# The third feed-forward's first product by seven block products instead of eight, with sums of weight blocks on GpSimd and sums of results when banks are read

## The chip, the cores and the metric

One core of one Trainium2 chip runs the whole program. The metric is the device time in microseconds (us) from start to end of one execution; the median of several executions counts. TensorE (PE in the profile) multiplies, with its weight loads listed apart as PEld; VectorE is DVE, ScalarE is ACT, GpSimd is POOL, and SyncE (SP) issues the loads from HBM. SBUF is the on-chip memory that all engines read, PSUM holds the eight banks into which TensorE writes its products.

## What is computed

Two layers over 256 context tokens and 256 latent tokens of 1024 features. Each layer is a feed-forward (FFN), a token mixer, and a second FFN; every part has a normalisation with shift, scale and gate in front. The change concerns the first FFN of the second layer, the third of four:

```python
def _modulated_norm(h, gain, shift, scale):
    return _rms_norm(h, gain) * (1.0 + scale) + shift

def _swiglu(h, w1, w2):
    a, b = jnp.split(h @ w1, 2, axis=-1)
    return (jax.nn.silu(a) * b) @ w2

for i in range(DEPTH):
    mx = (cond_x @ ada_w[i] + ada_b[i]).reshape(n_batch, 3, 3, 1, d)
    x = x + FFN_RESIDUAL * mx[:, 0, 2] * _swiglu(
        _modulated_norm(x, norm_g[i, 0], mx[:, 0, 0], mx[:, 0, 1]), ffn_w1[i, 0], ffn_w2[i, 0])
    ...
```

`w1` has 1024 rows and 2 x 2816 columns, so `h @ w1` gives 22 blocks of 128 columns for `a` and 22 for `b`. Inputs and weights are fp32.

## The kernel before

**Tiling.** Activations lie with features on the 128 partitions and all 512 tokens in a row: context in columns 0 to 255 (`CTX`), latent in 256 to 511 (`LAT`). The normalised input `H` is eight such chunks (k = 0 to 7). To keep fp32 accuracy each operand of a product is split into a rounded part "hi" and a rest "lo", and each product of two chunks is three matmuls: hi by hi, hi by lo, lo by hi (`mm3`, L292). A pair of outputs (`pa` for a block of `a`, `pb` for the same block of `b`, one PSUM bank each) takes 2 x 8 chunks x 3 = 48 matmuls of 512 columns (`ffn1_pairs`, L996).

**Weights.** `plan_weights` (L306) lists all weight loads and units in the order of use. SyncE loads tiles of 1024 rows by 256 columns into two pools of two buffers (`raw` and `ub`). `_split` (L447) makes a unit's hi by a ScalarE copy and its lo by a VectorE subtraction, four chunks (128x512) at a time. `w_ahead` (L483) is a task that keeps `LOOK` = 4 units split ahead of use. A unit of the FFN's first product is eight chunks, so a pair costs four copies and four subtractions.

**Evacuation.** `ffn_evac` (L871) reads a finished pair: silu of `pa` on ScalarE, times `pb` on VectorE, a rounded copy on ScalarE, the rest on VectorE. The result chunks `G` are the inputs of the second product (`out_blocks`, L1053), which adds each output block to the residual by VectorE.

**Order of the work.** An FFN runs in three parts of 6, 8 and 8 pairs, each followed by its share of the second product (`ffn`, L1102). The first two pairs of part 0 run as two halves by token group (`halves_first`, L1014), context columns first, because the normalisation of the latent half (`norm_half`, L856, and `h_chunks`, L817) ends later. A recording scheduler (`Sched`, L69) fixes the order of the instructions on every engine: each engine's queue is in program order, and tasks such as weight splits, evacuations and `ada_gen` (L682, the modulation vectors: 16 steps for each vector, here first eight VectorE steps, then eight ScalarE steps with seven GpSimd additions) are put in between matmuls by a clock that the scheduler keeps from its own costs. All recorded vector, scalar and GpSimd instructions carry line L184, the matmuls L284 and the transposes L289. In the names of the profile `u` is any tile of a pool of 76 buffers of 128x512 fp32, `mm` a PSUM bank, `raw` and `ub` loaded weights, `cc` the conditioning vector of `ada_gen`.

Of the kernel before, what the change touches and what calls it, by code (L numbers as in the profile page):

```python
# [213 lines left out]
class Kernel:  # L214
# [3 lines left out]
    LAG = (0.0, 2000.0)  # L218

    def __init__(self, tc, a, out, dbg, stack):  # L220
        self.s = Sched()
# [49 lines left out]

    def mm(self, out, lhsT, rhs, start=True, stop=True, tp=None, ns=None):
        kw = {} if tp is None else {"tile_position": tp}
# [10 lines left out]
        self.nc.tensor.matmul(out, lhsT, rhs, start=start, stop=stop, **kw)  # L284
        self.s.tick(ns)
# [6 lines left out]
    def mm3(self, ps, w, h, nk, sl=ALL, ks=None, start=True, stop=True):  # L292
# [4 lines left out]
        for i, k in enumerate(ks):  # L297
            if h is self.H:
                self.h_wait(k, sl)
            wh, wl = whi[k // 4][:, k % 4, :], wlo[k // 4][:, k % 4, :]  # L300
            self.mm(ps[:, sl], wh, hhi[k][:, sl], start=(start and i == 0), stop=False)
# [4 lines left out]
    def plan_weights(self):  # L306
# [13 lines left out]
        def unit(r, views, shape):  # L320
            for i in r:
                self.raws[i]["left"] += 1
            self.units.append({"r": r, "views": views, "shape": shape, "w": None})

# [8 lines left out]
        def ffn1(w1, p0, n):  # L333
# [33 lines left out]
        for l in range(2):  # L367
            for j in range(2):
                w1, w2 = a["ffn_w1"][l, j], a["ffn_w2"][l, j]
                for p0, n in self.parts:  # L370
                    if first:
                        ffn1(w1, 3, 3)
                        first = False
                    else:
                        ffn1(w1, p0, n)
# [71 lines left out]
    def _split(self):  # L447
        un = self.units[self.u_split]
        nc = self.nc
        tiles = [self.raws[i]["tile"] for i in un["r"]]  # L450
        nk, w = un["shape"]
        hi, lo = [], []
        if w == 512:
# [27 lines left out]
        self.u_split += 1  # L481

    def w_ahead(self):  # L483
# [333 lines left out]
    def h_chunks(self, hf, l, slot, ks, pace=None):  # L817
# [16 lines left out]
        for k in ks:  # L834
# [9 lines left out]
            f = None  # L844
            if k % 2:
                f = self.u()
# [9 lines left out]
    def norm_half(self, hf, sq, l, slot):  # L856
# [7 lines left out]
        if hf == "x":  # L864
            self.tables("silu")
            self.norming = self.urgent = self.lo_mix = False
            if (l, slot) == (0, 2):
                self.ada_pause = self.ada_hold = False


    def ffn_evac(self, pa, pb, sl):  # L871
# [230 lines left out]
    def ffn(self, l, j, sl, nxt, start=False):  # L1102
        v = 8 if j else 2
        for pi, (p0, n) in enumerate(self.parts):
            self.G = ([], [])
            if pi == 2 and (l, j) == (0, 0):
                self.ada_hold = True
            if pi == 0:
# [15 lines left out]
            else:
                self.ffn1_pairs(n, sl)
            last = pi == 2
# [848 lines left out]
    def run(self, upto=None):  # L1975
        self.upto = upto
        nc = self.nc
        self.acc = self.rs = None
        self.table = None
# [65 lines left out]
```

## Time and profile before

| | us |
|---|---|
| median of 3 runs (lowest, highest) | 1926.26 (1923.22, 1930.32) |
| the profiled execution, its own time | 1926.65 |
| span of its trace | 1924.9 |
| the third FFN's stretch with 512 columns at a time | 1232 to 1553 |

The profiled execution lies 0.39 us above the median, and its span covers all but 1.75 us of its time. In the views, a row of the timeline gives start, duration, engine, line, operation, output and input tiles, the count of merged instructions and, in brackets, the idle time before them and who ended it. A row by windows gives the length of the window, and for each engine its busy time and count of instructions, then the granted TensorE clock. A row of groups gives busy time, mean duration in ns, and the idle time before the instructions.

### The profile page before, as it was taken

The numbers are of one execution on the slowest core, as the hardware profiler recorded it, in microseconds if no ns is written. First come the engines' busy times: TensorE is split into PE (matmuls) and PEld (weight loads), VectorE is DVE, ScalarE is ACT, GpSimd is POOL, SyncE is SP. The second block draws the span as 40 slices with busy tenths as digits, with TensorE's granted clock in tenths as the row PEclk, the third lists the DMA queues.
The fourth block names the chain that finished last, engine by engine and source line by source line (L and its number), as shares of the span: only waits on it lengthen the run. The fifth ranks groups of instructions, "written<-read, shape, count | busy, mean of one in ns | idle before, by whom it ended". The sixth has DMA issues, their size and how long they took to land.

```text
span 1924.9 us, 28979 instructions
## 1 busy us (share of the span) xinstructions
PE 1865.4 (97%) x10719; PEld 1526.7 (79%) x10719; DVE 1282.2 (67%) x2124; ACT 965.4 (50%) x2106; POOL 643.6 (33%) x594
## 2 busy tenths in 40 slices
PE   8999999999999999999999999999999999899998
PEld 5878888897776666788888889888888898687887
DVE  4887877755977965478787786655433355956565
ACT  4544534457566455465445444533422248866553
POOL 3343433344546435354344333311200047230000
PEclk8999999999999998999999999999999999999999
DMA  9655554413322242444555454455323425126551
GB/s 290 211 184 194 179 175 153 129 46 125 94 67 83 69 162 83 151 157 157 193 187 170 159 197 147 142 175 187 119 91 102 131 67 110 45 67 184 199 197 66
DMA packets 238708, 271.70 MB, mean 141 GB/s; under 512 B 12343, under 2 KB 189135, under 8 KB 238567
## 3 DMA queue, kind: packets, MB, share of 16 engines
q1 hardware_dynamic: 237703, 269.15, 43.2%
q8 instruction: 84, 1.38, 0.3%
q10 hardware_dynamic: 720, 0.59, 0.1%
q14 instruction: 57, 0.47, 0.1%
q0 software_dynamic: 144, 0.11, 0.0%
HBM read 259.32 MB, written 10.49 MB: 140 GB/s over the span
## 4 chain that ended last, share of the span: by engine, by line
PE 56%; DVE 7%; ACT 4%; issue 2%; DMA 1%; POOL 1%; DVEq 0%; ACTq 0%; POOLq 0%
PE mm L284 55%; DVE u L184 6%; ACT u L184 3%; PE mm L289 1%; POOL u L184 1%; DMA raw<-in_ffn_w 0%; DVE st L184 0%; DVE big L184 0%; DMA ub<-in_ffn_w 0%; DMA u<-XD 0%; DVE ub L184 0%; ACT L184 0%; ACT ub L184 0%; ACT sc L184 0%; DVEq L184 0%
## 5 line engine op out<-in xcount | busy, mean ns | idle before, releaser
L284 PE MATMUL mm<-u 128*128 128x512 f32 (+4 forms) x9480 | 1777.0, 353 | 25.3 <-POOL u L184 9.9
L284 PEld LDWEIGHTS mm<-u 128*128 128x128 f32 (+1 forms) x9480 | 1457.4, 185 | 329.3 <-issue 39.6
L184 POOL TENSOR_TENSOR u<-u 128x512 f32<-128x512 f32 (+4 forms) x386 | 426.1, 1110 | 916.4 <-ACT u L184 869.8
L184 ACT ACTIVATE u<-u 128x512 fp32r<-128x512 f32 (+8 forms) x361 | 171.0, 485 | 450.5 <-DVE u L184 435.9
L184 ACT ACTIVATE u<-mm 128x128 f32<-128x128 f32 (+5 forms) x382 | 151.4, 412 | 252.3 <-PE mm L284 169.9
L184 DVE TENSOR_TENSOR u<-raw,u 128x512 fp32r<-128x512 f32 (+2 forms) x270 | 218.3, 849 | 63.2 <-ACT u L184 63.1
L184 DVE SCALAR_TENSOR_TENSOR u<-u,cc 128x512 f32<-128x512 f32 x196 | 222.5, 1135 | 10.1 <-DMA u<-in_ada_w 6.9
L184 DVE TENSOR_TENSOR u<-ub,u 128x512 fp32r<-128x512 f32 x252 | 199.1, 832 | 29.6 <-ACT u L184 29.5
L184 ACT ACTIVATE u<-raw 128x512 fp32r<-128x512 f32 (+1 forms) x372 | 206.3, 607 | 18.7 <-DMA raw<-in_ffn_w 11.8
L184 ACT ACTIVATE u<-u,cc 128x512 f32<-128x512 f32 x224 | 151.7, 711 | 112.4 <-DMA u<-in_ada_w 108.5
L184 POOL TENSOR_TENSOR u<-raw,u 128x512 fp32r<-128x512 f32 x98 | 129.6, 1347 | 141.8 <-ACT u L184 109.4
L184 ACT ACTIVATE u<-ub 128x512 fp32r<-128x512 f32 (+1 forms) x282 | 156.4, 609 | 18.4 <-DVE u L184 8.2
L184 DVE TENSOR_TENSOR u<-u,mm 128x512 f32<-128x512 f32 x66 | 45.2, 685 | 163.3 <-PE mm L284 156.9
L184 DVE TENSOR_TENSOR u<-u 128x512 fp32r<-128x512 f32 (+5 forms) x158 | 98.3, 622 | 66.0 <-ACT u L184 63.3
L184 DVE SCALAR_TENSOR_TENSOR u<-mm,mod,u 128x256 f32<-128x256 f32 x168 | 74.6, 478 | 93.1 <-PE mm L284 92.9
L184 DVE SCALAR_TENSOR_TENSOR u<-u,mod 128x256 f32<-128x256 f32 (+1 forms) x140 | 87.4, 675 | 27.4 <-ACT u L184 27.1
L184 ACT ACTIVATE u<-u,mod 128x256 fp32r<-128x256 f32 (+1 forms) x124 | 56.0, 501 | 54.4 <-DVE u L184 53.3
L289 PE MATMUL mm<-ident,u 128*128 128x128 f32 (+3 forms) x361 | 56.3, 289 | 22.4 <-ACT u L184 11.7
L184 DVE SCALAR_TENSOR_TENSOR u<-mm,cw,u 128x510 f32<-128x510 f32 (+1 forms) x96 | 71.3, 743 | 8.5 <-ACT u L184 6.6
L289 PEld LDWEIGHTS mm<-ident,u 128*128 128x128 f32 (+3 forms) x361 | 42.8, 148 | 37.9 <-ACT u L184 18.8
L184 DVE TENSOR_TENSOR u<-mm,u 128x256 f32<-128x256 f32 (+2 forms) x102 | 41.6, 419 | 34.7 <-PE mm L284 15.8
L184 DVE SCALAR_TENSOR_TENSOR u<-u,aS,mm 128x128 f32<-128x128 f32 x96 | 31.6, 345 | 25.1 <-PE mm L284 24.5
(120 smaller groups left out, 601.7 us busy)
## 6 DMA issues: line engine op xcount, KB each, us to landing
u<-in_ada_w SPq DMA_DIRECT2D x256, 256.0 KB, 5.7
ub<-in_ffn_w SPq DMA_DIRECT2D x60, 1024.0 KB, 5.5
raw<-in_ffn_w SPq DMA_DIRECT2D x58, 1024.0 KB, 5.3
raw<-in_dn_w_in SPq DMA_DIRECT2D x16, 1024.0 KB, 5.7
ub<-in_ada_w SPq DMA_DIRECT2D x12, 512.0 KB, 7.4
ub<-in_ffn_w SPq DMA_DIRECT2D x6, 768.0 KB, 4.7
raw<-in_ffn_w SPq DMA_DIRECT2D x6, 768.0 KB, 5.2
raw<-in_dn_w_out SPq DMA_DIRECT2D x4, 1024.0 KB, 6.5
```

What stands on the lines that cost most here:

```text
L184: r = f(*a, **k)
L284: self.nc.tensor.matmul(out, lhsT, rhs, start=start, stop=stop, **kw)
L289: self.nc.tensor.transpose(out, in_, self.ident[:k, :k])
```

## The change

For 20 of the 22 pairs of the third FFN (all but the two of `halves_first`) the pair's product is seen as two by two blocks: weights a1, a2 (contraction chunks 0 to 3 and 4 to 7 of the `a` block) and b1, b2, inputs H0 and H1 (the same chunk halves) for context c and latent x. Eight block products are replaced by seven, in Winograd's form. The weight forms are a1, b1+b2 (S1), a2, S1-a1 (S2), a2-S2 (S4), a1-b1 (S3) and b2; the four sums are made by GpSimd, once for every pair, and every form is split into hi and lo by ScalarE and VectorE. The input forms T are made once in `h_forms`: T(0) = H0x - H0c, T(1) = H1x - T(0), T(2) = H1x - H0x, T(3) = H1c - T(1), for four chunk pairs, with their own hi and lo. Each block product is 4 chunks x 3 = 12 matmuls of 256 columns, so a pair takes 84 of them instead of 48 of 512.

Some products belong to more than one result. So the bank half that holds such a sum is copied to SBUF by ScalarE when it is right for one result (`keep`, four copies of 128x256 for a pair), and accumulation goes on in the same bank half. `fast_evac` adds the kept halves (`ta`, `tb`) to the banks with two VectorE additions, and then does silu, product, copy and rest, as a task that yields between its steps. Look-ahead stays at `LOOK` = 4, where a form counts 0.5. The normalised input is also kept in fp32 (`Hf`): ScalarE writes it for all chunks instead of the odd ones.

```diff
+    FAST = {(1, 0)}
+    FORMS = ("A11", "S1", "A12", "S2", "S4", "S3", "A22")
...
+        def ffn1fast(w1, p0, n):
+            for p in range(p0, p0 + n, 2):
+                r = [cols(w1, 0, 8, 128 * p), cols(w1, 0, 8, F + 128 * p)]
+                for i in range(2):
+                    st = {"i": i}
+                    for f in self.FORMS:
+                        unit(r, [], (4, 128))
+                        self.units[-1].update(form=f, st=st, size=0.5)
...
+    def _split_form(self, un, tiles):
+        nc, st, f = self.nc, un["st"], un["form"]
+        cs = slice(128 * st["i"], 128 * st["i"] + 128)
+        (a1, a2), (b1, b2) = [(t[:, 0:4, cs], t[:, 4:8, cs]) for t in tiles]
+        def put(name, x, y, op):
+            st[name] = self.u((128, 4, 128))
+            nc.gpsimd.tensor_tensor(out=st[name], in0=x, in1=y, op=op)
+        if f == "A11":
+            put("S1", b1, b2, ALU.add)
+            put("S2", st["S1"], a1, ALU.subtract)
+        elif f == "A12":
+            put("S4", a2, st["S2"], ALU.subtract)
+            put("S3", a1, b1, ALU.subtract)
+        src = {"A11": a1, "A12": a2, "A22": b2}[f] if f[0] == "A" else st[f]
+        hi, lo = self.u((128, 4, 128), F32R), self.u((128, 4, 128), F32R)
+        self.act(out=hi, in_=src, func=AF.Copy)
+        nc.vector.tensor_tensor(out=lo, in0=src, in1=hi.bitcast(F32), op=ALU.subtract)
...
-            if self.u_split >= self.u_use + self.LOOK or self.urgent and self.u_split > self.u_use and len(self.hready) < 8:
+            if self.ahead() >= self.LOOK or self.urgent and self.u_split > self.u_use and len(self.hready) < 8:
...
-            if k % 2:
+            if (l, 0) in self.FAST and slot == 0:
+                if hf == "c":
+                    self.Hf[k] = self.u()
+                self.act(out=self.Hf[k][:, sl], in_=t[:, sl], func=AF.Identity, bias=B)
+                f = self.Hf[k] if k % 2 else None
+            elif k % 2:
...
+    def h_forms(self):
+        nc = self.nc
+        for k in range(4):
+            x, y = self.Hf[k], self.Hf[k + 4]
+            t, v = self.u(), self.u()
+            sub = lambda e, o, a, b: e.tensor_tensor(out=o, in0=a, in1=b, op=ALU.subtract)
+            sub(nc.vector, t[:, CTX], x[:, LAT], x[:, CTX])
+            sub(nc.vector, t[:, LAT], y[:, LAT], t[:, CTX])
+            sub(nc.gpsimd, v[:, CTX], y[:, LAT], x[:, LAT])
+            sub(nc.vector, v[:, LAT], y[:, CTX], t[:, LAT])
+            parts = []
+            for i, z in enumerate((t, v)):
+                yield self.at(z)
+                hi, lo = self.u(dt=F32R), self.u(dt=F32R)
+                self.act(out=hi, in_=z, func=AF.Copy)
+                yield self.at(hi)
+                sub(nc.gpsimd if i else nc.vector, lo, z, hi.bitcast(F32))
+                parts += [(hi, lo)]
+            self.T.append(parts)
+        self.Hf = {}
...
+    def fast_pairs(self, n):
...
+            block(pb[:, LAT], H(0, CTX))
+            keep(ta[:, CTX], pb[:, LAT])
+            block(pa[:, LAT], T(0))
+            keep(tb[:, LAT], pa[:, LAT])
+            block(pa[:, CTX], H(1, CTX), False)
+            block(pb[:, LAT], T(1), False)
+            keep(ta[:, LAT], pb[:, LAT])
+            block(pa[:, LAT], H(1, LAT), False)
+            block(pb[:, LAT], T(2), False)
+            keep(tb[:, CTX], pb[:, LAT])
+            block(pb[:, CTX], T(3), False)
+            t = self.fast_evac(pa, pb, ta, tb)
+            next(t)
+            self.s.add(t)
+    def fast_evac(self, pa, pb, ta, tb):
...
+        nc.vector.tensor_tensor(out=ta, in0=pa, in1=ta, op=ALU.add)
+        yield self.at(ta)
+        self.act(out=ta, in_=ta, func=AF.Silu)
+        nc.vector.tensor_tensor(out=tb, in0=pb, in1=tb, op=ALU.add)
+        yield self.at(ta, tb)
+        nc.vector.tensor_tensor(out=tb, in0=ta, in1=tb, op=ALU.mult)
+        yield self.at(tb)
+        self.act(out=ghi, in_=tb, func=AF.Copy)
+        yield self.at(ghi)
+        nc.vector.tensor_tensor(out=glo, in0=tb, in1=ghi.bitcast(F32), op=ALU.subtract)
```

Up to the third FFN and behind it the order on every engine is the one of before. Within it TensorE gets 720 more matmuls, VectorE 116 more instructions, ScalarE 156 and GpSimd 88.

On TensorE, from the latent half of the first two pairs to the end of part 0, first before:

```order
L284 MATMUL mm<-u 128x256 x67
L284 MATMUL mm<-u 128x512 x178
L284 MATMUL mm<-u,ones_87 32x512 x2
L284 MATMUL mm<-u 128x512 x16
L289 MATMUL mm<-ident,u 128x128 x4
```

and now (the first 67 of the 267 are the same as before):

```order
L289 MATMUL mm<-u 128x256 x267
L289 MATMUL mm<-u,ones_87 32x512 x2
L289 MATMUL mm<-u 128x256 x32
L294 MATMUL mm<-ident,u 128x64 x4
L289 MATMUL mm<-u 128x256 x101
L289 MATMUL mm<-u 128x512 x144
```

The four pairs that were 192 matmuls of 512 columns are 336 of 256; the 144 behind them are part 0 of the second product.

The second block of the first fast pair on TensorE takes T(0), chunk by chunk; bank `mm_12334` is its `pa`, `u_12203` and `u_12204` are S1's hi and lo, and `u_12386` and `u_12387` the hi and lo of T's last chunk:

```order
L289 MATMUL mm_12335<-u_11838,u_12186 128x256
L289 MATMUL mm_12334<-u_12167,u_12203 128x256
L289 MATMUL mm_12334<-u_12168,u_12203 128x256
L289 MATMUL mm_12334<-u_12167,u_12204 128x256
L289 MATMUL mm_12334<-u_12277,u_12203 128x256
L289 MATMUL mm_12334<-u_12278,u_12203 128x256
L289 MATMUL mm_12334<-u_12277,u_12204 128x256
L289 MATMUL mm_12334<-u_12369,u_12203 128x256
L289 MATMUL mm_12334<-u_12370,u_12203 128x256
L289 MATMUL mm_12334<-u_12369,u_12204 128x256
L289 MATMUL mm_12334<-u_12386,u_12203 128x256
L289 MATMUL mm_12334<-u_12387,u_12203 128x256
```

Before, `pa` of that pair took H's chunks here, which the pairs before it had already used.

On VectorE, the instructions behind the last one of the normalisation (`u_11867`, or `u_11872` now), before:

```order
L184 TENSOR_TENSOR u_12166<-raw_11546,u_12165 128x512
L184 TENSOR_TENSOR u_12170<-raw_11546,u_12169 128x512
L184 TENSOR_TENSOR mod1_5_195<-mm_12176,bT_176 128x8
L184 TENSOR_SCALAR u_12182<-u_11799,cc_91 128x512
L184 TENSOR_TENSOR u_12206<-u_12205,mm_11970 128x512
L184 TENSOR_TENSOR u_12208<-u_12206,u_12207 128x512
```

and the last twelve of the 37 that now stand from there up to the lo of T's last chunk, `u_12387`:

```order
L184 TENSOR_TENSOR u_12354<-u_11832 128x256
L184 TENSOR_TENSOR u_12354<-u_11876,u_12354 128x256
L184 TENSOR_TENSOR u_12355<-u_11876,u_12354 128x256
L184 SCALAR_TENSOR_TENSOR u_12207<-u_12261,cc_91,u_12207 128x512
L184 SCALAR_TENSOR_TENSOR u_12207<-u_12298,cc_91,u_12207 128x512
L184 SCALAR_TENSOR_TENSOR u_12207<-u_12343,cc_91,u_12207 128x512
L184 TENSOR_TENSOR u_12370<-u_12354,u_12369 128x512
L184 TENSOR_TENSOR u_12377<-u_11843 128x256
L184 TENSOR_TENSOR u_12377<-u_11888,u_12377 128x256
L184 TENSOR_TENSOR u_12378<-u_11888,u_12377 128x256
L184 SCALAR_TENSOR_TENSOR u_12207<-u_12361,cc_91,u_12207 128x512
L184 TENSOR_TENSOR u_12387<-u_12377,u_12386 128x512
```

The 37 are 12 half-wide subtractions of `h_forms` and 4 lo parts of T, 8 lo parts of weight forms, 4 instructions of the two evacuations of `halves_first`, 8 steps of `ada_gen` (all that one modulation vector has on VectorE) and one of 8 columns. GpSimd has 14 in the same place: 4 half-wide and 4 wide ones of `h_forms` and 6 sums of weight blocks.

More of the change, by code (lines that the diff above doesn't have):

```diff
@@ L269, in tables, with mm @@
             self.nc.scalar.preload_act_table_set({"exp": "natural_log_exp_and_others", "silu": "silu_and_others"}[name])
-    def mm(self, out, lhsT, rhs, start=True, stop=True, tp=None, ns=None):
-        kw = {} if tp is None else {"tile_position": tp}
+    def mm(self, out, lhsT, rhs, start=True, stop=True, tp=None, ns=None, **kw):
+        if tp is not None:
+            kw["tile_position"] = tp
         if ns is None:
@@ L322, in unit @@
                 self.raws[i]["left"] += 1
-            self.units.append({"r": r, "views": views, "shape": shape, "w": None})
+            self.units.append({"r": r, "views": views, "shape": shape, "w": None, "form": None, "size": 1.0})
         def cols(mat, r0, nk, c0, w=256):
@@ L451, in _split @@
         nk, w = un["shape"]
+        if un["form"]:
+            self._split_form(un, tiles)
+            return
         hi, lo = [], []
@@ L481, in _split, with ahead @@
         self.u_split += 1
+    def _split_form(self, un, tiles):
[15 more added lines that the diff above has]
+        nc.vector.tensor_tensor(out=lo, in0=src, in1=hi.bitcast(F32), op=ALU.subtract)
+        un["w"] = (hi, lo)
+        for i in un["r"]:
+            self.raws[i]["left"] -= 1
+            self.raws[i]["until"] = max(self.s.free[e] for e in ("scalar", "gpsimd", "vector"))
+        self.u_split += 1
+    def ahead(self):
+        return sum(u["size"] for u in self.units[self.u_use:self.u_split])
     def w_ahead(self):
@@ L1003, in ffn1_pairs, with block, keep @@
                 self.w_done()
+    def fast_pairs(self, n):
+        H = lambda i, sl: [tuple(p[4 * i + k][:, sl] for p in self.H) for k in range(4)]
+        T = lambda i: [tuple(p[:, 256 * (i % 2):256 * (i % 2) + 256] for p in self.T[k][i // 2]) for k in range(4)]
+        nc = self.nc
+        for _ in range(n):
+            pa, pb = self.mmt(), self.mmt()
+            ta, tb = self.u(), self.u()
+            self.s.until(lambda: len(self.T) == 4)
+            def block(out, mov, first=True):
+                kw = {} if first else {"skip_group_check": True}
+                hi, lo = self.w_get()
+                for k in range(4):
+                    hh, hl = mov[k]
+                    self.mm(out, hi[:, k, :], hh, start=(first and k == 0), stop=False, **kw)
+                    self.mm(out, hi[:, k, :], hl, start=False, stop=False, **kw)
+                    self.mm(out, lo[:, k, :], hh, start=False, stop=(k == 3), **kw)
+                self.w_done()
+            def keep(dst, src):
+                self.act(out=dst, in_=src, func=AF.Copy)
+            block(pb[:, LAT], H(0, CTX))
[12 more added lines that the diff above has]
+            self.s.add(t)
@@ new lines, in fast_evac @@
+    def fast_evac(self, pa, pb, ta, tb):
+        nc = self.nc
+        slot, done = len(self.G[0]), self.Gset
+        ghi, glo = self.u(dt=F32R), self.u(dt=F32R)
+        self.G[0].append(ghi)
+        self.G[1].append(glo)
+        yield 0
+        nc.vector.tensor_tensor(out=ta, in0=pa, in1=ta, op=ALU.add)
[8 more added lines that the diff above has]
+        nc.vector.tensor_tensor(out=glo, in0=tb, in1=ghi.bitcast(F32), op=ALU.subtract)
+        done.add(slot)
@@ L1977, in run @@
         nc = self.nc
-        self.acc = self.rs = None
+        self.acc = self.rs = self.G = None
+        self.Hf = {}
         self.table = None
```

21 lines of the change are left out of this document (17 added, 4 removed).

## The prediction

> **What bounds the kernel now.** I read the stretch of the third FFN by windows first, cut at its parts: pairs of part 0, second product of part 0, pairs of part 1 (three windows), second product, pairs of part 2 (two), and the start of the last second product.
>
> ```profile
> core 0: us, PE busy (x) PEld busy (x) DVE busy (x) ACT busy (x) POOL busy (x), PEclk, DMA share, GB/s
> 1232.00:1276.00 44.00, 44.00 (x195) 35.50 (x194) 20.30 (x30) 17.88 (x33) 9.65 (x7) 1.00 0.53 180
> 1276.00:1309.00 33.00, 33.00 (x149) 27.05 (x148) 23.02 (x41) 14.12 (x27) 7.35 (x5) 1.00 0.51 175
> 1309.00:1353.00 44.00, 44.00 (x196) 35.23 (x195) 22.61 (x35) 13.67 (x24) 4.83 (x4) 1.00 0.51 174
> 1353.00:1376.00 23.00, 23.00 (x104) 18.79 (x104) 10.21 (x12) 9.60 (x17) 8.74 (x6) 1.00 0.50 168
> 1441.00:1485.00 44.00, 44.00 (x196) 36.44 (x195) 14.76 (x25) 10.54 (x19) 0.00 (x0) 1.00 0.34 111
> 1485.00:1529.00 44.00, 44.00 (x196) 36.44 (x195) 15.16 (x24) 13.26 (x24) 0.00 (x0) 1.00 0.34 110
> ```
>
> TensorE never waits there, at full clock; the other engines are a third to two thirds busy, and GpSimd works only while the modulation vectors run, up to 1376. So a matmul less is time less, as long as the rest keeps up. Next the timeline of TensorE, for the spacing of matmuls, and for the wait in front of the stretch:
>
> ```profile
> 1209.83 0.28 PE L284 MATMUL mm<-u 128*128 128x256 f32 x1
> 1222.48 1.09 PE L284 MATMUL mm<-u 128*128 128x256 f32 x7 [0.73 <-POOL u L184]
> 1223.89 16.49 PE L284 MATMUL mm<-u 128*128 128x256 f32 x103
> 1277.72 46.54 PE L284 MATMUL mm<-u 128*128 128x512 f32 x204
> 1566.45 13.78 PE L284 MATMUL mm<-u 128*128 128x256 f32 x112
> ```
>
> A matmul of 512 columns comes every 46.54/204 = 0.228 us. Of 256 columns it is (13.78 - 0.28)/111 = 0.1216 us when the last one's own length is taken off: more than half of 0.228, so half of the saving in columns goes into the fixed part of each matmul.
>
> **The product itself.** A pair was 48 x 0.228 = 10.94 us and becomes 84 x 0.1216 = 10.21 us. That is 0.73 us for each of 20 pairs, 14.6 us in all (12 at 13.78/112 = 0.123 us, 17 at 0.120). Nothing in the change can give more than this.
>
> In the Trainium skill, page "TensorE: Matmul & The Clock Gate", section "Back-to-back issue gap", a lone matmul is given as columns over 2.4 plus 2.5 ns, 109 and 216 ns. By these figures the product would save 24 us (an estimate from that page); the rows above measure this very stream, so the sum goes by them.
>
> **What the other engines pay for a pair.** Prices are in the groups of instructions, for 1353 to 1376 (with GpSimd at work), then for 1441 to 1529 (without):
>
> ```profile
> L184 DVE TENSOR_TENSOR u<-ub,u 128x512 fp32r<-128x512 f32 x6 | 6.3, 1095 | 1.8 <-ACT u L184 1.8
> L184 POOL TENSOR_TENSOR u<-u 128x512 f32<-128x512 f32 x6 | 8.7, 1457 | 12.7 <-ACT u L184 12.4
> ```
>
> ```profile
> L184 DVE TENSOR_TENSOR u<-raw,u 128x512 fp32r<-128x512 f32 x17 | 10.8, 685 | 0.0
> L184 DVE TENSOR_TENSOR u<-u,mm 128x512 f32<-128x512 f32 x7 | 4.8, 687 | 46.0 <-PE mm L284 46.0
> L184 ACT ACTIVATE u<-ub 128x512 fp32r<-128x512 f32 x14 | 7.8, 616 | 0.0
> L184 ACT ACTIVATE u<-mm 128x512 f32<-128x512 f32 x8 | 4.8, 598 | 40.4 <-PE mm L284 40.4
> L184 ACT ACTIVATE u<-u 128x512 fp32r<-128x512 f32 x7 | 4.4, 632 | 39.4 <-DVE u L184 39.4
> ```
>
> and half-wide ones of ScalarE in the timeline:
>
> ```profile
> 1216.71 2.77 ACT L184 ACTIVATE u<-u,mod 128x256 fp32r<-128x256 f32 x6 [1.40 <-DVE u L184]
> ```
>
> VectorE had 6 such instructions for a pair (4 lo parts, product, rest), and gets 11: 7 lo parts, 2 additions, product, rest, 11 x 0.687 = 7.56 us. GpSimd gets 4 sums. What these cost VectorE is the point: the same subtraction takes 1095 ns where GpSimd works and 685 where it doesn't. Six subtractions lost 6 x 0.41 = 2.46 us beside six GpSimd instructions, 0.41 us for each of them, while VectorE was busy 10.21 of 23 us; for a VectorE that is never idle that scales to 0.41 x 23/10.21 = 0.93. So VectorE needs 7.56 + 4 x 0.41 to 4 x 0.93 = 9.2 to 11.3 us for a pair, against 10.21 on TensorE: it stands at the edge. ScalarE needs 7 x 0.616 + 4 half-wide copies of 2.77/6 = 0.46 + 0.598 + 0.632 = 7.4 us and stays under; GpSimd 4 x 1.457 = 5.8.
>
> **The wait for T.** This is the largest term. The timelines of VectorE and of GpSimd where the latent normalisation ends, and two prices from the page's groups:
>
> ```profile
> 1218.71 2.37 DVE L184 SCALAR_TENSOR_TENSOR u<-u,mod 128x256 fp32r<-128x256 f32 x4 [0.18 <-ACT u L184]
> 1224.89 0.48 DVE L184 TENSOR_SCALAR u<-u,cc 128x512 f32<-128x512 f32 x1
> 1229.74 0.74 DVE L184 SCALAR_TENSOR_TENSOR u<-u,cc 128x512 f32<-128x512 f32 x1
> ```
>
> ```profile
> 1221.71 0.72 POOL L184 TENSOR_TENSOR u<-u 128x256 fp32r<-128x256 f32 x1 [1.31 <-ACT u L184]
> ```
>
> ```profile
> L184 POOL TENSOR_TENSOR u<-raw,u 128x512 fp32r<-128x512 f32 x98 | 129.6, 1347 | 141.8 <-ACT u L184 109.4
> L184 DVE TENSOR_TENSOR u<-mm,u 128x256 f32<-128x256 f32 (+2 forms) x102 | 41.6, 419 | 34.7 <-PE mm L284 15.8
> ```
>
> VectorE ends the normalisation at 1218.71 + 2.37 = 1221.08. The first fast pair starts on TensorE 67 matmuls behind 1223.89, at 1232.03, and wants T's last chunk 21 matmuls later, at 1234.6. Ahead of that chunk's lo part and with it VectorE has 37 instructions: 12 x 0.419 + 16 x 0.687 + 7 x 0.74 + 0.48 + about 0.16 = 21.8 us, so not before 1242.9. Eight of them are steps of the modulation, which stand in this queue among T's chunks, so T waits for them too. That alone is a wait of 8.3 us on TensorE. GpSimd has 14 instructions beside it, worth 10 + 4 x 0.72/1.347 = 12 wide ones, 12 x 0.41 to 12 x 0.93 = 5 to 11 us more for VectorE. The wait is 8 to 19 us; I take 13, the nearest to the lower price for GpSimd, because part of its work comes behind T's chunks.
>
> A wait of that length also costs clock. The windows around the longest idle time near the last FFN show it:
>
> ```profile
> 1722.00:1726.00 4.00, 1.41 (x8) 0.94 (x6) 1.74 (x5) 2.19 (x5) 0.01 (x1) 1.00 0.80 262
> 1726.00:1732.00 6.00, 4.61 (x16) 3.01 (x15) 4.21 (x9) 5.15 (x10) 3.29 (x4) 0.72 0.00 0
> ```
>
> After 2.6 us of idle TensorE the granted clock is 0.72 over 6 us, 1.7 us of work lost. I take 2 us (0 to 3.4, two such stretches).
>
> **The smaller terms.** ScalarE writes eight more fp32 chunks in the normalisation, 8 x 2.77/6 = 3.7 us, on a chain where it alternates with VectorE: 0 to 3.7 us, I take 2. In part 1 VectorE has 8 x 7.56 and 4 steps of the modulation, 63.5 us, less 8 forms split ahead (5.5); GpSimd has 32 sums and 7 additions, of which about 6 lie ahead. That is 58 + 33 x 0.41 to 33 x 0.93 = 72 to 89 us, against 8 x 10.21 - 1.5 = 80 us on TensorE to the last form: 0 to 9, I take 4. Part 2 without the modulation: 55 + 26 x 0.41 to 26 x 0.93 = 66 to 79, nothing; I take 0.5 (0 to 2). Part 0 is behind T's wait, during which everything gets ahead: nothing. At each part's end the second product wants the last G after 5 to 7 steps of 3 x 0.228 us, 3.4 to 4.8 us. Addition, product, copy and rest are 3 x 0.687 + 0.632 = 2.7 us with up to eight weight splits queued in front on VectorE: 0 to 4 for a part, I take 4 in all (0 to 10). The kept halves: the bank half that T(1) fills is wanted again by T(2) one block (1.46 us) later, and the copy (0.46) may stand behind one split copy (0.616) on ScalarE: covered; without that cover up to 0.2 us a pair, I take 1 (0 to 4). The weight tiles are freed later, after 14 forms instead of 3 or 4 units, but then 14 more forms, 14 x 1.46 = 20 us, are still to come from the other two buffers; SyncE's loads fit in, nothing (0 to 2).
>
> **The sum.** 13 + 2 + 2 + 4 + 0.5 + 4 + 1 = 26.5 us of new waits against 14.6 us saved: 12 us slower than the profiled execution's 1926.65, 1938.6; less the 0.4 by which that lies above the median, 1938.
>
> **Rivals.** *VectorE keeps up.* T's wait is near its lower bound, 9, GpSimd costs VectorE the 0.41, and the parts run without a wait: 9 + 1 + 1 + 1 - 14.6 = -3, 1923, no slower than before. It decides at 10.21 us of VectorE a pair, and at how much of GpSimd's work falls beside T. For it: 685 ns is kept wherever GpSimd rests. Against it: 1095.
>
> *GpSimd stops VectorE in full.* Each sum costs VectorE its whole 1.347 us: 9 x 0.687 + 4 x 1.347 = 11.6 us a pair, over TensorE's 10.21; part 1 would wait 11 us, T 24, the part ends 8; with the other small terms 34 us more than is saved, 1960. In the Trainium skill, page "SBUF — State Buffer", section "Who interferes with whom", a VectorE instruction with two SBUF inputs and a GpSimd instruction that reads SBUF exclude each other, the second waiting for the whole of the first. The trace bears this out only in part: beside 1457 ns of GpSimd the mean loss is 0.41 us, not 1.35.
>
> *T is no wait.* Were the 37 instructions done by 1234.6, the 14.6 us would stay but for the small terms: 1914. They would have 13.5 us; their bare durations are 21.8, so only little speaks for this.
>
> **How the numbers follow.** The forecast has 0.50 and its own range, 1930 to 1948; VectorE keeps up 0.28; GpSimd in full 0.12; T no wait 0.10. With 0.5% of the time, 9.6 us, as about what a measurement of this kernel can tell from no change, the bounds are 1916.6 and 1935.9. Faster: the last rival, 0.10. Same: the first rival and the lower third of the forecast, 0.28 + 0.15 = 0.43. Slower: the rest, 0.47. The range from 1919 to 1953 leaves out the last rival and most of the second, 0.2.
>
> **What would show it.** In the profile of the changed kernel: matmuls of 256 columns at 0.12 us; one idle time of TensorE of 8 to 19 us near 1234, released by VectorE, and a clock under 1 right behind it; VectorE's lo parts at about 1.0 us in the parts, with VectorE over nine tenths busy in part 1; waits of TensorE at the parts' starts and ends. Wrong would be: no wait above 5 us at T, or VectorE's lo parts near 685 ns beside GpSimd, or fast pairs closer together than 10.1 us.

## The result, and the profile after

The changed kernel took 1973.22 us (median of 4 runs, 1969.86 to 1973.76), the kernel before beside it 1927.06 us (1923.22 to 1930.32): 1.0248 times, with a 95% interval of 1.0226 to 1.0270. So it is slower, as forecast, but by 46 us instead of 12, and outside the range that was given. The profiled execution took 1973.32 us, its span 1971.5 us, 46.6 us more than before.

Where the time went is read from the stages. These are the lengths in us between the first matmuls of the stages in the two traces; the second product stands behind its part, and what comes behind the third FFN is equally long in both.

| kernel | pairs, part 0 | product | pairs, part 1 | product | pairs, part 2 | sum |
|---|---|---|---|---|---|---|
| before | 44.76 | 33.26 | 90.71 | 43.52 | 87.04 | 299.29 |
| after | 74.39 | 35.04 | 100.52 | 43.55 | 92.23 | 345.73 |

The windows of after at the same stages (columns as in the prediction):

```profile
core 0: us, PE busy (x) PEld busy (x) DVE busy (x) ACT busy (x) POOL busy (x), PEclk, DMA share, GB/s
1232.00:1306.00 74.00, 50.56 (x343) 45.18 (x342) 59.62 (x72) 36.73 (x74) 37.21 (x24) 0.82 0.39 118
1306.00:1341.00 35.00, 34.26 (x153) 27.39 (x152) 26.34 (x39) 14.19 (x24) 19.31 (x13) 1.00 0.54 179
1341.00:1442.00 101.00, 88.99 (x688) 83.85 (x685) 86.43 (x100) 56.43 (x114) 53.23 (x34) 0.98 0.41 129
1442.00:1485.00 43.00, 43.00 (x192) 35.61 (x191) 20.72 (x33) 10.94 (x18) 9.57 (x7) 1.00 0.23 74
1485.00:1577.00 92.00, 84.36 (x670) 81.01 (x669) 73.52 (x87) 49.60 (x102) 40.24 (x26) 1.00 0.34 107
```

Before, TensorE was busy in every one of these stages without a gap. Now it is idle for 23 us of part 0, 12 of part 1 and 8 of part 2, while no other engine is full over a whole part. Waits, then, not work. The first ones stand in the timeline of TensorE, inside the second block of the first seven-block pair. (That pair starts at 1232.09, 64 matmuls behind the four small transposes in front of it, not 67 as before. Its first block and the first chunk of T(0) run without a wait.)

```profile
1235.47 0.38 PE L289 MATMUL mm<-u 128*128 128x256 f32 x1 [1.43 <-ACT u L184]
1241.59 0.80 PE L289 MATMUL mm<-u 128*128 128x256 f32 x2 [5.73 <-DVE u L184]
1246.96 0.58 PE L289 MATMUL mm<-u 128*128 128x256 f32 x1 [4.57 <-ACT u L184]
1250.94 0.80 PE L289 MATMUL mm<-u 128*128 128x256 f32 x2 [3.40 <-DVE u L184]
1252.46 0.58 PE L289 MATMUL mm<-u 128*128 128x256 f32 x1 [0.72 <-ACT u L184]
1253.46 0.80 PE L289 MATMUL mm<-u 128*128 128x256 f32 x2 [0.42 <-DVE u L184]
1255.26 8.53 PE L289 MATMUL mm<-u 128*128 128x256 f32 x48 [1.00 <-ACT u L184]
```

The first six are the wait for T, 16.3 us together: for the second, third and fourth chunk of T(0) once for the hi by ScalarE, once for the lo by VectorE. The seventh, 1.00 us, stands ahead of the third block and is of another kind, which part 2 shows alone. The 48 matmuls behind it take 8.53 us instead of 6.01, as the clock is low (0.70 from 1255 to 1265).

In part 2 nothing of that kind is left, and still every pair waits. TensorE there, and ScalarE's first rows in part 2:

```profile
1485.82 2.80 PE L289 MATMUL mm<-u 128*128 128x256 f32 x22
1489.09 6.01 PE L289 MATMUL mm<-u 128*128 128x256 f32 x48 [0.47 <-ACT u L184]
1495.57 4.57 PE L289 MATMUL mm<-u 128*128 128x256 f32 x36 [0.47 <-ACT u L184]
1500.61 1.57 PE L289 MATMUL mm<-u 128*128 128x256 f32 x11 [0.47 <-ACT u L184]
```

```profile
1487.22 0.38 ACT L184 ACTIVATE u<-mm 128x256 f32<-128x256 f32 x1 [5.11 <-PE mm L289]
1487.50 0.62 ACT L184 ACTIVATE u<-u 128x512 fp32r<-128x512 f32 x1
1488.66 0.38 ACT L184 ACTIVATE u<-mm 128x256 f32<-128x256 f32 x1 [0.53 <-PE mm L289]
```

The pattern is 4 blocks, a wait, 3 blocks, a wait, from pair to pair; the waits stand ahead of blocks 3 and 7. Ahead of block 3 the chain is plain: TensorE ends block 2 at 1485.82 + 2.80 = 1488.62, ScalarE copies its half of the bank from 1488.66 to 1489.04, TensorE goes on at 1489.09. Blocks 3 and 7 write the context half of a bank whose latent half, written by the block right ahead, is just being kept. In the program's order the first matmul of these blocks waits for ScalarE. From start to start block 2 then lasts 2.07 us and block 3 1.53, instead of 1.44 each, as a stream of matmuls that stops also loses its overlap: 0.72 us, twice in a pair.

### The profile page after: what moved, and what is told of

It is laid out like the page before. It is cut to its first block, busy times and chain, and to the rows that moved or that the text cites. A ratio compares the mean times of both kernels' runs of the same rounds, so it can differ in the third digit from the quotient of the medians.

```text
span 1971.5 us, 30945 instructions
## 1 busy us (share of the span) xinstructions
PE 1867.6 (95%) x11439; PEld 1555.7 (79%) x11439; DVE 1419.2 (72%) x2240; ACT 1036.0 (53%) x2262; POOL 782.1 (40%) x682
## 4 chain that ended last, share of the span: by engine, by line
PE 52%; DVE 9%; ACT 5%; issue 3%; DMA 1%; POOL 1%; DVEq 0%; ACTq 0%; POOLq 0%
PE mm L289 51%; DVE u L184 8%; ACT u L184 5%; PE mm L294 1%; POOL u L184 1%; DMA ub<-in_ffn_w 1%; DMA raw<-in_ffn_w 0%; DVE st L184 0%; DVE big L184 0%; DMA u<-XD 0%; ACT L184 0%; DVE ub L184 0%; DVEq L184 0%; DVE mod L184 0%; ACTq L184 0%
## 5 line engine op out<-in xcount | busy, mean ns | idle before, releaser
L289 PE MATMUL mm<-u 128*128 128x512 f32 (+5 forms) x10200 | 1780.6, 340 | 69.4 <-ACT u L184 40.6
L289 PEld LDWEIGHTS mm<-u 128*128 128x128 f32 (+2 forms) x10200 | 1488.4, 186 | 348.0 <-ACT u L184 61.8
L184 POOL TENSOR_TENSOR u<-u 128x512 f32<-128x512 f32 (+5 forms) x394 | 439.0, 1120 | 716.1 <-ACT u L184 668.6
L184 ACT ACTIVATE u<-u 128x512 fp32r<-128x512 f32 (+8 forms) x469 | 235.4, 517 | 395.2 <-DVE u L184 375.0
L184 ACT ACTIVATE u<-mm 128x128 f32<-128x128 f32 (+4 forms) x442 | 170.5, 399 | 279.6 <-PE mm L289 198.5
L184 DVE TENSOR_TENSOR u<-u 128x512 fp32r<-128x512 f32 (+4 forms) x274 | 218.5, 813 | 78.0 <-ACT u L184 72.1
L184 POOL TENSOR_TENSOR u<-raw,u 128x512 fp32r<-128x512 f32 (+1 forms) x108 | 144.9, 1363 | 146.1 <-ACT u L184 108.2
L184 ACT ACTIVATE u<-ub 128x512 fp32r<-128x512 f32 (+1 forms) x272 | 153.1, 610 | 38.2 <-PE mm L289 14.6
L184 DVE TENSOR_TENSOR u<-mm,u 128x256 f32<-128x256 f32 (+2 forms) x142 | 68.7, 493 | 35.4 <-PE mm L289 15.9
L184 DVE TENSOR_TENSOR u<-u,mm 128x512 f32<-128x512 f32 x46 | 31.5, 685 | 49.4 <-PE mm L289 48.4
L184 POOL TENSOR_TENSOR u<-ub,u 128x512 fp32r<-128x512 f32 (+1 forms) x40 | 57.2, 1446 | 18.0 <-ACT u L184 9.7
```

What stands on the lines that cost most here:

```text
L184: r = f(*a, **k)
```

## The experiments

For the runs that leave part 0 alone, "16 pairs" are those of parts 1 and 2. All ratios are to the kernel before. Stage lengths of the profiled executions in us, counted as above:

| kernel | pairs, part 0 | product | pairs, part 1 | product | pairs, part 2 |
|---|---|---|---|---|---|
| new order of blocks | 69.55 | 34.41 | 96.13 | 43.55 | 84.85 |
| modulation held | 64.78 | 34.90 | 103.25 | 45.37 | 92.23 |
| new order, sums on VectorE | 62.72 | 34.97 | 83.86 | 43.55 | 80.63 |
| 16 pairs, old order | 44.76 | 33.26 | 102.85 | 43.55 | 92.25 |
| 16 pairs, new order | 44.76 | 33.26 | 99.29 | 43.55 | 84.85 |
| the same, modulation stopped | 44.76 | 33.26 | 89.44 | 50.03 | 87.40 |
| the same, without the sums | 44.76 | 33.26 | 85.87 | 43.55 | 80.63 |
| the same, sums on VectorE | 44.76 | 33.26 | 86.10 | 47.00 | 80.63 |
| 16 pairs, old order, sums on VectorE | 44.76 | 33.26 | 96.36 | 48.19 | 92.44 |
| 16 pairs, new order, adds on VectorE too | 44.76 | 33.26 | 85.83 | 47.74 | 80.63 |

**The order of the blocks.** Before each block that takes the other half of a kept bank, a block of the other bank is put in between; the forms and sums follow.

```diff
-    FORMS = ("A11", "S1", "A12", "S2", "S4", "S3", "A22")
+    FORMS = ("A11", "S1", "S2", "A12", "S3", "S4", "A22")
...
-            block(pa[:, CTX], H(1, CTX), False)
             block(pb[:, LAT], T(1), False)
             keep(ta[:, LAT], pb[:, LAT])
-            block(pa[:, LAT], H(1, LAT), False)
+            block(pa[:, CTX], H(1, CTX), False)
             block(pb[:, LAT], T(2), False)
             keep(tb[:, CTX], pb[:, LAT])
+            block(pa[:, LAT], H(1, LAT), False)
             block(pb[:, CTX], T(3), False)
```

> The changed kernel with its seven blocks in another order (the first H(0) block, then T(1), H(1) on the context columns, T(2), H(1) on the latent columns ...), so that between each half that ScalarE keeps and the next block in that half's bank there stands a block of the other bank. The sums, copies and the wait at the start stay. Theory A, the bank: TensorE's first matmul into one half of a bank waits until ScalarE has ended its copy of the other half, 0.73 us twice in each of 20 pairs; then a pair falls from 11.54 to about 10.1 us and the kernel from 1973 to about 1944 us (1938 to 1950). Rival B, the copies are simply late on ScalarE (its queue holds the rounded copies of weights too): the wait moves one block on and most of it stays, 1966 to 1975 us. Rival C, the 0.47 us rows are the cost of taking up after another form of matmul and have nothing to do with ScalarE: no change, 1970 to 1976 us.

Measured: 1955.54 us, 1.0165 (1.0142 to 1.0188), 18 us less than after. None of the three had it: the even waits are gone, which B and C excluded, but a third of the 29 us stays. TensorE in part 2 of this version:

```profile
1508.98 20.72 PE L289 MATMUL mm<-u 128*128 128x256 f32 x168 [1.14 <-ACT u L184]
1530.05 10.36 PE L289 MATMUL mm<-u 128*128 128x256 f32 x84 [0.34 <-ACT u L184]
1541.37 3.86 PE L289 MATMUL mm<-u 128*128 128x256 f32 x30 [0.96 <-ACT u L184]
```

Whole pairs run through now. What is left are uneven waits, still put down to ScalarE; part 2 is at 84.85 us, where 8 x 84 matmuls at 0.120 us are 80.6.

**The pairs of part 0 left as they were.** `fast_pairs` and `ffn1fast` are used in parts 1 and 2 alone.

```diff
-            pairs = self.fast_pairs if (l, j) in self.FAST else lambda n: self.ffn1_pairs(n, sl)
+            pairs = self.fast_pairs if pi and (l, j) in self.FAST else lambda n: self.ffn1_pairs(n, sl)
```

> The changed kernel with the seven block products in parts 1 and 2 alone (16 pairs); the four pairs of part 0 are the ordinary ones of before, so that nothing of the third FFN waits for T. Theory A: the wait at T and the low clock behind it (about 18 us), part 0's late copies and its four dear pairs go, 30 us of part 0's stage in all; the 16 pairs that stay cost 11.54 us each against 10.9 before (10 us), and part 1 its late weights (8 us): 1943 to 1949 us. Rival D, the work on VectorE before T (the latent norm, modulation steps) only moves to part 1 and holds its pairs up there: 1955 us or more.

Measured: 1944.18 us, 1.0097 (1.0066 to 1.0128). Part 0 and its product are exactly at 44.76 and 33.26 us again, part 2 is unchanged at 92.25, part 1 at 102.85 instead of 100.52. So the 30 us of part 0 belong to its own pairs, and hardly anything moves on. The time agrees with theory A, and D is out.

**Both.** The two edits together.

> Both of the foregoing: the new order of the blocks, and the ordinary pairs in part 0. Theory A: 16 pairs at 10.1 us against 10.9 gain 13 us on the kernel before, less 0 to 9 us of late weights in part 1: 1914 to 1923 us, the first version faster than the kernel before. Rival B (the copies late on ScalarE): about the time of the ordinary order with part 0 left alone less 5 us, 1938 to 1946 us. Rival D (part 0's work only moves): 1930 to 1950 us.

Measured: 1933.30 us, 1.0052 (1.0031 to 1.0072): 10 us above what A expected and 5 below B; it lies in D's range, but the version before this one has shown that part 0's work does not move on. The bank was not all of it. Part 1 has 99.29 us. Something is late there that the waits for the bank had covered.

**No sums.** In the version with both edits the blocks' raw halves stand in for the sums, so GpSimd has 64 instructions less; all else stays.

```diff
-            st[name] = self.u((128, 4, 128))
-            nc.gpsimd.tensor_tensor(out=st[name], in0=x, in1=y, op=op)
+            st[name] = x
```

> The version with the new order in parts 1 and 2 (16 pairs), with the sums of weight blocks left out: the blocks' raw halves stand in for S1 to S4, so GpSimd does 64 sums less, and the output is not the reference's. Theory G, contention (VectorE's low parts at about 1.05 us instead of 0.69 while GpSimd works, and so ScalarE, whose next copy waits for VectorE): part 1 falls from 99 to 81 to 86 us and part 2 from 85 to 81 to 82 us, the kernel to 1912 to 1920 us. Rival H, VectorE has too many instructions in part 1 whatever GpSimd does (modulation steps, sums of results): part 1 stays over 92 us and the kernel at 1926 to 1933 us.

Measured: 1910.11 us, 0.9941 (0.9916 to 0.9965). Part 1 falls to 85.87 and part 2 to 80.63 us, its bare matmuls. That is what theory G expected, at a time 2 us below its range, and H is out: VectorE's own number of instructions is no obstacle. But leaving the sums out takes away two things at once, what GpSimd does beside VectorE and the time that the blocks wait for the sums themselves.

**The sums on VectorE.** The same version as in "both", with all its work, and the sums moved:

```diff
-            nc.gpsimd.tensor_tensor(out=st[name], in0=x, in1=y, op=op)
+            nc.vector.tensor_tensor(out=st[name], in0=x, in1=y, op=op)
```

> The same version with the four sums of a pair on VectorE instead of GpSimd (64 x 0.69 us). Theory G: VectorE loses the slowing (some 17 us of part 1 by its means of 0.92, 1.13 and 1.49 us against 0.69 and 0.75) and gains 32 x 0.69 = 22 us there; in part 1 it comes out about even, 95 to 102 us, in part 2 at 84 to 90 us; the kernel at 1930 to 1942 us. Rival H, the number of VectorE's instructions alone decides: part 1 rises by 22 us and part 2 by up to 15, 1955 us or more. Rival I, the path through GpSimd (1.3 to 1.8 us for a sum, two in a row) is what the blocks wait for: 1915 to 1925 us.

Measured: 1915.46 us, 0.9980 (0.9965 to 0.9994). Giving VectorE 64 instructions more made the kernel 18 us faster. It came out at rival I's time, below what G expected. The time alone doesn't part the two, as the path through GpSimd goes with the contention; but G's cause is at work, as VectorE's groups in part 2 (1452 to 1532 us) show. First with the sums on GpSimd, and behind them the row of that window:

```profile
L184 DVE TENSOR_TENSOR u<-u 128x512 fp32r<-128x512 f32 x35 | 37.2, 1090 | 1.5 <-ACT u L184 1.5
L184 DVE TENSOR_TENSOR u<-ub,u 128x512 fp32r<-128x512 f32 x12 | 13.4, 1119 | 1.8 <-ACT u L184 1.8
L184 DVE TENSOR_TENSOR u<-raw,u 128x512 fp32r<-128x512 f32 x12 | 12.2, 1032 | 0.9 <-ACT u L184 0.9
L184 DVE TENSOR_TENSOR u<-u 128x512 f32<-128x512 f32 x6 | 5.2, 865 | 0.0
```

```profile
1452.00:1532.00 80.00, 77.36 (x623) 75.68 (x622) 73.71 (x81) 43.54 (x92) 42.44 (x27) 1.00 0.30 99
```

and with the sums on VectorE:

```profile
L184 DVE TENSOR_TENSOR u<-u 128x512 fp32r<-128x512 f32 x32 | 21.8, 685 | 5.9 <-ACT u L184 5.9
L184 DVE TENSOR_TENSOR u<-ub,u 128x512 fp32r<-128x512 f32 x14 | 9.5, 685 | 1.6 <-ACT u L184 1.6
L184 DVE TENSOR_TENSOR u<-raw,u 128x512 fp32r<-128x512 f32 x14 | 9.3, 686 | 2.1 <-ACT u L184 2.1
L184 DVE TENSOR_TENSOR u<-ub 128x512 f32<-128x512 f32 x8 | 5.4, 681 | 0.0
```

```profile
1452.00:1532.00 80.00, 80.00 (x631) 78.38 (x631) 67.08 (x110) 46.58 (x96) 0.00 (x0) 1.00 0.42 136
```

Beside GpSimd the 65 instructions of the first four rows lost 35 x 0.405 + 12 x 0.434 + 12 x 0.347 + 6 x 0.18 = 24.6 us against 0.685 each. Over 27 GpSimd instructions that is 0.91 us for each, of the 42.44/27 = 1.57 us that one lasts. VectorE does such a sum itself in 0.68 us: the helper costs it more than the work. Only instructions with both inputs in SBUF were slowed: the 14 additions of that window that read one input from a PSUM bank kept 0.679 us.

The waits of the version with GpSimd's sums part the two theories. In that window of part 2 ScalarE waited 23.1 us for VectorE and never for GpSimd, and VectorE never for GpSimd: there it is G. In part 1 (1312 to 1411) ScalarE's rounded copies also waited 6.9 us for GpSimd, so there rival I has a share.

**The old order, without GpSimd.** This holds the bank alone against the version just told: the old order of the blocks, the 16 pairs, the sums on VectorE.

> The seven blocks in the changed kernel's own order, in parts 1 and 2 alone, with the four sums of a pair on VectorE instead of GpSimd (so that GpSimd slows nothing): against the version with the new order and the same sums on VectorE, 1915 us, only the order of the blocks differs. Theory A, the bank: TensorE waits 0.73 us twice a pair again, 16 x 1.46 = 23 us: 1936 to 1941 us, and in part 2 a pair of 11.5 us against 10.1. Rival B, what cost in the changed kernel was ScalarE's lateness, which the sums on VectorE have taken away: 1914 to 1924 us.

Measured: 1940.27 us, 1.0097 (1.0078 to 1.0116), 25 us above the new order. In part 2, 92.44 against 80.63 us, 1.48 us for a pair, and TensorE has the even pattern again with GpSimd at rest:

```profile
1475.28 4.57 PE L289 MATMUL mm<-u 128*128 128x256 f32 x36 [0.47 <-ACT u L184]
1480.33 6.01 PE L289 MATMUL mm<-u 128*128 128x256 f32 x48 [0.47 <-ACT u L184]
1486.82 4.57 PE L289 MATMUL mm<-u 128*128 128x256 f32 x36 [0.47 <-ACT u L184]
```

So the wait for the bank is a cost of its own, and the order of the blocks removes it. B is out.

**The modulation steps ahead of T.** The changed kernel, with `ada_pause` set from the end of the latent normalisation until the T are queued.

```diff
             if (l, 0) in self.FAST and slot == 0:
+                self.ada_pause = True
                 self.s.add(self.h_forms())
...
         self.Hf = {}
+        self.ada_pause = False
```

> The changed kernel, with the modulation steps of the next layer's norms held back from the end of the latent norm until the nine sums T are queued, so that 29 instead of 37 instructions stand on VectorE between the norm's last chunk and the last sum. Theory E, T is late by VectorE's queue: the wait of the first fast pair falls by the 6 to 9 us of these steps, to 1963 to 1968 us. Rival F, T is late by the copies and results that its own sums wait for, and VectorE would have idled there: no change, 1970 to 1976 us. The copies for the blocks (0.73 us twice a pair) stay in both.

Measured: 1969.47 us, 1.0242 (1.0216 to 1.0267). The rows of its wait for T:

```profile
1237.07 0.38 PE L289 MATMUL mm<-u 128*128 128x256 f32 x1 [0.45 <-ACT u L184]
1241.18 0.80 PE L289 MATMUL mm<-u 128*128 128x256 f32 x2 [3.73 <-DVE u L184]
1246.68 0.58 PE L289 MATMUL mm<-u 128*128 128x256 f32 x1 [4.70 <-ACT u L184]
1247.68 0.80 PE L289 MATMUL mm<-u 128*128 128x256 f32 x2 [0.42 <-DVE u L184]
1250.67 1.52 PE L289 MATMUL mm<-u 128*128 128x256 f32 x3 [2.20 <-ACT u L184]
```

The pieces are 11.5 us together instead of 16.3, 4.8 less, where theory E expected 6 to 9; part 0 is 9.6 us shorter. But part 1 and its product are 4.6 us longer, where the steps that were held can have come, and the two medians differ by 4 us only. E is right on the cause of the wait, too high on its size and wrong on the total.

**Both remedies in all three parts.** The new order and the sums on VectorE, part 0 included.

> The changed kernel with both remedies, the new order of the blocks and the sums on VectorE, in all three parts, so that only the wait of part 0 for T and the norm's extra chunks are left of what the changed kernel lost. Against the version without part 0 (1915 us): theory A, the wait for T (some 17 us and a low clock behind it of 2 us) less 4 x 0.8 us, and nothing else: 1929 to 1937 us. Rival L, the wait for T is itself made by GpSimd's sums of the first weight blocks on the same buffers' path: 1914 to 1922 us.

Measured: 1929.76 us, 1.0039 (1.0024 to 1.0054), in theory A's range. Its waits for T:

```profile
1236.37 0.79 PE L289 MATMUL mm<-u 128*128 128x256 f32 x2 [5.80 <-DVE u L184]
1243.08 0.58 PE L289 MATMUL mm<-u 128*128 128x256 f32 x1 [5.92 <-ACT u L184]
1244.84 0.80 PE L289 MATMUL mm<-u 128*128 128x256 f32 x2 [1.18 <-DVE u L184]
1247.78 0.58 PE L289 MATMUL mm<-u 128*128 128x256 f32 x1 [2.14 <-ACT u L184]
1249.13 0.79 PE L289 MATMUL mm<-u 128*128 128x256 f32 x2 [0.77 <-DVE u L184]
```

Together 15.8 us: taking the weight sums from GpSimd and giving them to VectorE leaves this wait nearly as it was, so L's time is out. As the sums now stand in VectorE's own queue ahead of T, what they had cost T from GpSimd isn't shown. The order of the blocks and the engine of the sums have taken the kernel from 1.0248 to 1.0039, and of what stays, part 0 with its product is 19.7 us longer than before.

**The price of narrow matmuls.** The kernel before, with the same 20 pairs as 96 matmuls of 256 columns each.

```diff
-    FAST = {(1, 0)}
+    FAST = set()
...
-                self.mm3(ps, self.w_get(), self.H, 8, sl)
+                if self.halve:
+                    w = self.w_get()
+                    for hs in (CTX, LAT):
+                        self.mm3(ps, w, self.H, 8, hs)
+                    w = None
+                else:
+                    self.mm3(ps, self.w_get(), self.H, 8, sl)
```

> The kernel before, with the 20 ordinary pairs of the third FFN computed as 96 matmuls of 256 columns each instead of 48 of 512; no sums, no seven blocks. It prices what a matmul costs beside its columns. Theory A (a matmul of 256 columns takes 120 ns with its weights, one of 512 takes 227): 20 x (96 x 0.120 - 48 x 0.227) = +12.6 us on the kernel before, 1935 to 1939 us. Rival (the 120 ns are a price of the blocks' form, or halving is free): within 3 us of the kernel before.

Measured: 1934.58 us, 1.0078 (1.0060 to 1.0095), 13 us above before, as theory A expected. Part 2 is one stream without a wait, 8 x 96 matmuls in 92.15 us, 0.1200 us each, where 8 x 48 of 512 columns took 87.04, 0.2267 us each. So a pair of 84 costs 10.08 us against 10.88, and the product alone saves 20 x 0.80 = 16 us.

**The modulation stopped in parts 1 and 2.** "Both", with the steps of `ada_gen` stopped while the 16 pairs run.

```diff
             while self.ada_pause and (h, k) == (0, 0):
                 yield 3000
+            while self.ada_stop:
+                yield 1000
...
+            self.ada_stop = (l, j) in self.FAST and pi > 0
```

> The version with the new order in parts 1 and 2, and the modulation steps of the next layer's norms stopped while the pairs of parts 1 and 2 run (they go on in the second products). Nothing is left out. Theory J, these steps fill VectorE (7 of 1.49 us and the adds on it) and ScalarE's queue in part 1: part 1 falls from 99 to 83 to 88 us, part 2 stays at 85 (it has none), and the kernel comes to 1917 to 1924 us, unless the held steps come due before the next norm. Rival K, they only pass their place to other work (part 2 without them is still 4 us over its matmuls, so part 1 without them might be at 85, but what is held back lands in part 2 or holds up the next norm): 1928 us or more.

Measured: 1930.09 us, 1.0053 (1.0029 to 1.0078). J is out. In the trace (an execution of 1940.40 us, 10 above the median) part 1 gains 9.9 us (3.7 of them are TensorE's matmuls for two modulation vectors, which leave it), the product behind it loses 6.5 and part 2 loses 2.6, as K has it: the steps only change their place.

**The modulation's additions on VectorE too.** The version with the sums on VectorE, where the seven GpSimd additions of part 1 go to VectorE as well.

```diff
-                eng = nc.vector if self.norming else nc.gpsimd
+                eng = nc.vector if self.norming or self.fast else nc.gpsimd
```

> The version with the new order and the sums on VectorE in parts 1 and 2, and the modulation steps' adds (7 in part 1, on GpSimd until now) on VectorE too while the pairs run, so that GpSimd does nothing in them. Theory G, GpSimd beside VectorE still costs part 1 some 5 us (sums of 1.12 and 0.84 us there against 0.68 in part 2): part 1 falls from 86.0 to 82 to 84 us, the kernel to 1911 to 1914 us. Rival H, the 7 adds more (4.8 us) on a VectorE that is 9/10 busy eat it up: 1914 to 1918 us.

Measured: 1917.78 us, 0.9981 (0.9964 to 0.9998). Not told apart from the version without this edit, and in rival H's range. Part 1 stays at 85.8 us, where theory G expected 82 to 84. TensorE also makes the matmuls of two modulation vectors around here, 90.71 less 8 x 10.88 = 3.7 us in part 1 before, 1.8 for each. One of them falls into part 1 in this trace and the other into the product, as in the version without this edit, so part 1 would take 80.6 + 1.8 = 82.5 us without a wait. It has 3.4 us of waits with this edit and 3.6 without. Whether the additions cost next to nothing on GpSimd, or as much there as on VectorE, this run doesn't part.

## Why the prediction was wrong

**The step that failed** is "The kept halves: ... covered; without that cover up to 0.2 us a pair, I take 1 (0 to 4)". It followed only the half that T(1) fills until T(2) takes the same half, one block on. Blocks 3 and 7 take the other half of the same bank at once, and the program's waits go by the bank. The prediction named the copies and their durations, and set them against the wrong next writer. It comes to 29 us: 20 pairs at the (92.23 - 80.63)/8 = 1.45 us of part 2. In the Trainium skill, page "PSUM — Partial Sum Buffer", section "Terms", TensorE's write and ScalarE's read may not meet in one bank and 32 partitions; with that rule read beside the list of blocks the term would have been there. No run here leaves the wait out, so that the bank itself needs it isn't shown; shown is that the program waits, and for how long.

The other terms, against the stages (part 0: 44.76, less 4 x 0.80 = 3.2 that the product saves, plus 4 x 1.45 = 5.8 for the bank, is 47.4, so 27.0 us are for all else; part 1 in the same way: 90.71 - 6.4 + 11.6, so 4.6; part 2: nothing. The matmuls of the modulation vectors also shift between the stages: some 1.2 us of them leave part 1, and half of that falls into part 0 and half into its product. So the waits are 26.4 us in part 0 and 5.8 in part 1):

- *The product*, 14.6 us saved (12 to 17): 16.0, by the narrow matmuls' 0.1200 us. Right.
- *T's wait*, 13 us (8 to 19): 16.3 us of idle time. With the slow restarts it is 19.6, at the upper end: the block that takes T(0) lasted from 1233.53 to 1255.26, 21.73 us instead of 1.44, of which 0.73 are the bank's. Its cause holds: holding eight modulation steps (5.7 us by the prediction's rows) shortened the idle time by 4.8. What was sized too low is, by the rows, GpSimd's price for VectorE, for which I took the lower one: a lo part of 0.69 us alone lasted up to 1.76 us there. That it comes chunk by chunk, for ScalarE and VectorE in turn, was not foreseen; the chain through both engines counts, not VectorE's queue alone.
- *The clock*, 2 us (0 to 3.4): 8.53 instead of 6.01 us for the next 48 matmuls, 2.5, at the granted 0.70. Right.
- *The norm's extra chunks*, 2 us: 1.1. From the norm's first matmul with the ones to the first of these pairs it is 1232.03 - 1190.90 = 41.13 us before and 1232.09 - 1189.90 = 42.19 now.
- *Part 0 behind T's wait: nothing*. Wrong, by about 4 us: 26.4 less 19.6 and 2.5 is 4.3. The largest of these waits is 3.32 us, ahead of 1283.67, and behind it the clock was low again, 0.81 from 1283 to 1292. ScalarE shows why:

```profile
1279.62 0.63 ACT L184 ACTIVATE u<-ub 128x512 fp32r<-128x512 f32 x1 [3.32 <-DVE u L184]
1281.92 0.63 ACT L184 ACTIVATE u<-u 128x512 f32<-128x512 f32 x1 [1.66 <-DVE u L184]
1282.45 0.37 ACT L184 ACTIVATE u<-mm 128x256 f32<-128x256 f32 x1
1282.72 0.62 ACT L184 ACTIVATE u<-u 128x512 fp32r<-128x512 f32 x1
1283.24 0.38 ACT L184 ACTIVATE u<-mm 128x256 f32<-128x256 f32 x1
```

  The silu (the second row) stands in ScalarE's queue ahead of the two kept copies and waits for VectorE's addition, which waits behind lo parts slowed by GpSimd. TensorE goes on when the second kept copy has ended, at 1283.62. So TensorE's wait is put down to ScalarE, and VectorE is its source.
- *Part 1*, 4 us (0 to 9): 5.8; *part ends*, 4 us: 1.2, at part 0 alone (35.04 - 33.26, less the shifted 0.6); *part 2*, 0.5: nothing. In sum near the forecast, but by luck: the bank's waits stretched a pair to 11.52 us, and so gave VectorE its time. (Part 1 also had eight VectorE steps of the modulation, not the four of the sum.) With these waits gone, the weight forms were late by 15 us in part 1 (99.29 against 80.6 + 3.7) and by 4.2 in part 2. That is why the new order alone won 18 us and not 29.
- *GpSimd's price for VectorE*, 0.41 to 0.93 us for a sum: 0.91. The rival "GpSimd stops VectorE in full" put 1.35, too much: VectorE was slowed for 0.91 of 1.57 us. (Its 11.6 us a pair also counts 9 of VectorE's 11 instructions; with all of them it would be 12.9.) In the Trainium skill, page "SBUF — State Buffer", section "Who interferes with whom", the one waits for the whole of the other; the trace agrees that VectorE loses time to GpSimd's sums, not that it loses all of theirs. But its consequence, that beside GpSimd's sums VectorE can't keep up with TensorE, did come true, and was hidden: without the bank's waits a pair of part 2 took 84.85/8 = 10.6 us, and 10.08 with the sums on VectorE.

Together the terms are 29.0 + 19.6 + 2.5 + 1.1 + 4.3 + 5.8 + 1.2 - 16.0 = 47.5 us; the spans differ by 46.6, since in this trace the norm began 1.0 us earlier than before. Of the 34 us that the forecast fell short, 28 are the bank's.

Of what would show it, the low clock at T, the 0.12 us and lo parts near 1.0 us came true, and T's wait in its range, though in six pieces and released by ScalarE as often as by VectorE; "over nine tenths busy in part 1" did not (86.43 of 101 us), because TensorE itself had become slower.

The fastest of these runs that leaves no work out, the new order and the sums on VectorE in parts 1 and 2, is at 0.9980 (0.9965 to 0.9994) of the kernel before: faster by 0.06% to 0.35%, where 16 pairs at 0.80 us would be 0.7%. In its trace the third FFN is 7.5 us shorter (4.6 in part 1, 6.4 in part 2, and 3.5 lost in the product between them, where one modulation vector's matmuls now fall), and the stretch behind it 2.9. That is 10 us, less 1.1 for the norm in front; the timed runs show less, and where the rest goes was not followed.

## What to carry to other kernels

When a partial sum is copied out while its bank goes on being used, list who next writes any part of that *bank*, and put a block of another bank in between: here 1.5 us a pair hung on the order of seven lines. A helper engine is free only if it doesn't slow the one that it helps: price it on both, and try the plain way, since VectorE did a sum in 0.68 us that on GpSimd cost it 0.91. When a large wait is removed, look at what it was covering before adding up the gain.

## What was not expected of the hardware

A wait that the rows of part 2 give as 0.47 us costs 0.72 from start to start: 48 matmuls between two waits take 6.01 us where 48 in the stream take 5.76, because the last one ahead of the stop shows its whole length, 0.28 us instead of 0.12, and the second one behind the stop comes 0.22 us after the first. Stages of the third FFN are equal to a few hundredths of a us from kernel to kernel (44.76, 33.26, 43.55, 80.63), but the traces of these kernels reach its first ordinary or fast pair of part 0 anywhere between 1223.3 and 1236.8 us. Gains of some us are therefore read from stages, and from medians only with several runs.
